# A two-layer decoder trunk on one core: six raw weight buffers, four lower ones, and a gate bias moved to another queue and to later steps

## The chip, the core and the metric

The kernel runs on one core of a Trainium2 chip. The metric is the device time of one execution in microseconds (us). The engines that matter here are TensorE (PE; its weight loads are PEld), VectorE (DVE), ScalarE (ACT), GpSimd (POOL) and SyncE (SP), which only issues DMAs. Each engine works through its own instructions in a fixed order; a DMA is issued by the queue of one of them, and an instruction that waits holds back everything behind it on its engine or queue.

## What is computed

Each of two layers normalises x (256 rows, 2048 columns), projects it with one wide matrix, feeds four branches, merges the branches under sigmoid gates and adds one output projection to x.

```python
for l in range(DEPTH):                                   # DEPTH = 2
    h = rms_norm(x, norm_g[l])
    proj = h @ w_in[l]                                   # 2048 -> 9 x 1024 + 2 x 512 + 64 + 8192
    (pv, pz, cq, ckv, kr, mz, cb, cc, cx, cz, xq, xz, gpre) = split(proj)
    y_pool = pool_mixer(pv, pool_w[l], pool_scale[l]) * silu(pz)
    y_mla  = mla_mixer(cq, ckv, kr, ...) * silu(mz)
    y_conv = conv_mixer(cb, cc, cx, conv_w[l]) * silu(cz)
    y_mem  = memory_xattn(xq, rms_norm(mem) @ w_mem_kv[l], ...) * silu(xz)
    gates  = sigmoid(gpre + gate_b[l])                   # four gates of 256 x 2048
    merged = sum(gates[:, :, i] * (y[i] @ w_branch[l, i]) for i in range(4))
    x = x + merged @ w_out[l]
```

All of it is float32. The weights are read once, and every 128 x 1024 chunk of them goes through the same preparation before TensorE uses it.

## The kernel before

**Chunks.** A weight chunk is 128 partitions by 1024 columns, 512 KB. `wchunks` (line 310) takes three buffers for it: `raw` (four of them), the upper part `hi` (five) and the lower part `lo` (five). SP loads `raw`, ScalarE rounds it into `hi` (L321), VectorE subtracts the two into `lo` (L322), and TensorE uses both parts with the activations, which are split in the same way. `tm_block` (activations as the stationary operand, L334 to L336) does three matmuls of 512 columns for each 128 rows of weight; `fm_block` and `fine_block` (weights stationary) do one of 512 columns for `hi` and one of 256 for `lo`. `fm_block` (L343) makes two 128-column halves from chunks of 256 columns by four k-tiles, and serves the projections mz and xz; `fine_block` (L373) makes one half from two chunks of 128 columns by eight k-tiles, and serves pv, pz, cc, cx, cb and cz (the names in `FINE`). A fine block's sum stands in one of two small PSUM banks, `ms`, until ScalarE has copied it out (`fmt`, L387).

**Order.** The program is written as if in one sequence; a scheduler turns it into an order for each engine, by priority and by when buffers come free. Within `tc.high_priority(n)` instructions are taken n places earlier than they stand. `lead[0]` is that n for the load, the cast and the subtraction of a chunk: `AHEAD` = 100, and `NEAR` = 40 in the stage described next. A buffer of a tag goes to the tiles of that tag one after the other, when an earlier tile's last reader is done.

**The stage of seven block products.** After the gates of the mla and mem branches the kernel computes the pool and conv branches out of 48 fine blocks (`pool_branch`, `conv_branch`). Between them it works off three other pieces of the input projection: the groups (0, 0), (0, 1) and (2, 0) of `SEVEN`, each 1024 columns of the pool or conv gate. A group is a 2 x 2 block product done with seven multiplications instead of eight (`seven`, L415). For each of eight pairs of row tiles it loads two raw chunks `ra` and `rb`, forms block differences in them in place (L457, L458, L467, L468), makes four pairs of `hi` and `lo` (casts L449, L456, L466, L476, subtraction L441), and issues seven products of three matmuls each (L432 to L434). `ra` and `rb` stay in their buffers until the last pairs that come from them are made. A group's sums fill three `acc` tiles and one `ms` bank. The generator yields after every product. Every fine block first calls `pull(RATE)` with RATE = 160/46, so three or four products are done ahead of each fine block; in the pool branch's output matmuls (`fm_tile`, L340 and L341) `pull(1)` asks for one. `drain` finishes what is left.

**End of a group.** When the last product is done, ScalarE and VectorE put the seven sums together (L485 to L492) and the generator yields True, which ends that pull. At the next pull it goes on with both halves of the group's bias: each loads 512 values of `gate_b`, broadcast to 128 rows, by SP into a `gb` tile (two buffers, L496), adds it on VectorE (L497), takes the sigmoid on ScalarE (L498), and stores the gate to DRAM by POOL's queue (`kept`, L499). `gates` later reads these back by POOL's queue (L979); the other twenty gate pieces are computed there with a `gb` load of their own on SP (L982). The tag `t2` has seven buffers of 128 x 512 for all kinds of short-lived tiles (`fmt`, `sg`, `c`, `u3`, `yp`, `mt` and others).

Of the kernel before, what the change touches and what calls it, by code (L numbers as in the profile page):

```python
# [10 lines left out]
F32 = mybir.dt.float32  # L11
F32R = mybir.dt.float32r
# [5 lines left out]
P = 128  # L18
AHEAD = 100
NEAR = 40  # L20
# [2 lines left out]
SEQUENCE = "A0 A1 F T0 F T1 S0 A2 F V0 T2 S1 A3 F V1 T3 S2 F V2 S3 F V3 X0 X1 F Y0 Y1 X2 X3 F Y2 Y3"  # L23
CK = 2
SCRATCH = 1024
FINE = ("pv", "pz", "cc", "cx", "cb", "cz")
D = 2048
S = 256
DEPTH = 2
# [2 lines left out]
KT = D // P  # L32
# [33 lines left out]
def weight_plan():  # L66
    plan, off = {}, 0

    def add(name, c0, n, nk, kt):
        nonlocal off  # L70
        plan[name, c0] = (off, n, nk, kt)
        off += P * kt * n

    def fm(name):
        if name in FINE:
            for b in range(8):
                add("in", OFF[name] + 128 * b, 128, 8, KT)
        else:
            for b in range(4):
                add("in", OFF[name] + 256 * b, 256, 4, KT)  # L80

    for e in range(4):
        add("mem_kv", 512 * e, 512, 2, KT)
    add("in", OFF["cq"], 512, 2, KT)
    for b in range(2):
        add("in", OFF["ckv"] + 288 * b, 288, 2, KT)
    for b in range(2):
        add("in", OFF["xq"] + 512 * b, 512, 2, KT)
    for hp in range(4):
        add("uq", 384 * hp, 384, 2, 4)  # L90
        add("ukv", 512 * hp, 512, 2, 4)
    for name in ("mz", "xz", "pv", "pz", "cc", "cx", "cb", "cz"):
        fm(name)
    for b in range(2):
        add("pool", 512 * b, 256, 4, 4)
    for bi in range(4):
        for e in range(4):
            if (bi, e // 2) not in SEVEN:
                add("in", OFF["gate"] + bi * D + 512 * e, 512, 2, KT)
            elif e % 2 == 0:  # L100
                add("in", OFF["gate"] + bi * D + 512 * e, 1024, 1, KT)
            add(f"br{bi}", 512 * e, 512, 2, 8)
    for e in range(4):
        add("out", 512 * e, 512, 2, KT)
    return plan, off
# [17 lines left out]
def tile_hybrid_trunk(  # L123
# [16 lines left out]
    def nm(s):  # L140
        uid[0] += 1
        return f"{s}{uid[0]}"
# [13 lines left out]
    def t2(s):  # L156
        return tp.tile([P, 512], F32, tag="t2", name=nm(s), bufs=7)
# [32 lines left out]
    def bcast_rows(v):  # L190
        return v.rearrange("(o n) -> o n", o=1).broadcast_to([P, v.shape[0]])
# [101 lines left out]
    def step():  # L293
        if background:
            run = background.pop(0)
            if run is not None:
                run()
# [7 lines left out]
            background.extend([None] * (delay - len(background)))  # L305
        background.extend(runs)

    stream, owed, lead = [], [0.0], [AHEAD]

    def wchunks(l, name, c0):  # L310
        off, n, nk, kt = plan[name, c0]
        m = nk * n
        for k0 in range(0, kt, nk):
            raw = wp.tile([P, 1024], F32, tag="raw", name=nm("raw"), bufs=4)
            hi = wp.tile([P, 1024], F32R, tag="hi", name=nm("hi"), bufs=5)
            lo = wp.tile([P, 1024], F32R, tag="lo", name=nm("lo"), bufs=5)
            o = off + P * n * k0
            step()
            with tc.high_priority(lead[0]):
                nc.sync.dma_start(raw[:, :m], weights[l, o : o + P * m].rearrange("(p m) -> p m", p=P))  # L320
                A.copy(hi[:, :m], raw[:, :m])  # L321
                V.tensor_tensor(lo[:, :m], raw[:, :m], hi[:, :m].bitcast(F32), ALU.subtract)  # L322
            yield k0, nk, kt, n, *(w[:, :m].rearrange("p (k n) -> p k n", n=n) for w in (hi, lo))
# [16 lines left out]
        T.matmul(ps[:, j, :], hi[:, k, n0 : n0 + P], o[:, half].rearrange("p a s -> p (a s)"), start=first, stop=False)  # L340
        T.matmul(ps[:, j, :S], lo[:, k, n0 : n0 + P], o[:, half, 0, :], start=False, stop=last)  # L341

    def fm_block(rhs, l, name, c0):  # L343
        ps = acc()
        for k0, nk, kt, n, hi, lo in wchunks(l, name, c0):
            for j in range(2):
                n0 = j * P
                for k in range(nk):
                    o = rhs[(k0 + k) // 2][:, k % 2].rearrange("p a s -> p (a s)")
                    T.matmul(ps[:, j, :], hi[:, k, n0 : n0 + P], o, start=k0 + k == 0, stop=False)  # L350
                for k in range(nk):
                    o = rhs[(k0 + k) // 2][:, k % 2, 0, :]
                    T.matmul(ps[:, j, :S], lo[:, k, n0 : n0 + P], o, start=False, stop=k0 + k == kt - 1)  # L353
        return ps


    def pull(n):
        owed[0] += n
        while stream and owed[0] >= 1:
            owed[0] -= 1  # L360
            done = next(stream[0], None)
            if done is None:
                stream.pop(0)
            if done:
                break

    def drain():
        while stream:
            owed[0] = 1000.0
            pull(0)  # L370
        owed[0] = 0.0

    def fine_block(rhs, l, c0):  # L373
        pull(RATE)
        ps = ms()
        for k0, nk, kt, n, hi, lo in wchunks(l, "in", c0):
            for k in range(nk):
                o = rhs[(k0 + k) // 2][:, k % 2].rearrange("p a s -> p (a s)")
                T.matmul(ps, hi[:, k, :], o, start=k0 + k == 0, stop=False)  # L379
            for k in range(nk):  # L380
                o = rhs[(k0 + k) // 2][:, k % 2, 0, :]
                T.matmul(ps[:, :S], lo[:, k, :], o, start=False, stop=k0 + k == kt - 1)  # L382
        return ps

    def fine_sum(dst, ps):
# [29 lines left out]
    def seven(l, bi, ep, h, sx):  # L415
# [5 lines left out]
        for u in range(8):  # L421
# [13 lines left out]

            def pair():
                hi = wp.tile([P, 1024], F32R, tag="hi", name=nm("hi"), bufs=5)
                return hi, wp.tile([P, 1024], F32R, tag="lo", name=nm("lo"), bufs=5)

            def lower(x, raw, cols):  # L440
                V.tensor_tensor(x[1][:, cols], raw[:, cols], x[0][:, cols].bitcast(F32), ALU.subtract)  # L441

            ra, rb = (wp.tile([P, 1024], F32, tag="raw", name=nm("raw"), bufs=4) for _ in range(2))
            with tc.high_priority(lead[0]):
                for i, r in enumerate((ra, rb)):
                    at = off + P * 1024 * (2 * u + i)
                    nc.sync.dma_start(r, weights[l, at : at + P * 1024].rearrange("(p m) -> p m", p=P))
                x = pair()
                A.copy(x[0][:, left], ra[:, left])  # L449
                lower(x, ra, left)  # L450
# [39 lines left out]
        V.tensor_tensor(c, c, bank[5], ALU.add)  # L490
        V.tensor_tensor(g[1][:, 0, :], c, bank[3], ALU.add)
        V.tensor_tensor(g[0][:, 1, :], u3, bank[4], ALU.subtract)  # L492
        yield True
        for i in range(2):
            gb = tp.tile([P, 512], F32, tag="gb", name=nm("gb"), bufs=2)
            nc.sync.dma_start(gb, bcast_rows(gate_b[l, c0 + 512 * i : c0 + 512 * (i + 1)]))  # L496
            V.tensor_tensor(g[i], g[i], gb.unsqueeze(1).broadcast_to([P, 2, 512]), ALU.add)  # L497
            A.activation(g[i], g[i], AF.Sigmoid)  # L498
            nc.gpsimd.dma_start(kept[bi, 2 * ep + i], g[i])  # L499

    def fm_sum(dst, ps):
        tmp = t2("fmt").rearrange("p (n s) -> p n s", n=2)
# [149 lines left out]
        return kT, vv  # L652

    def silu_half(z, i, h, l, c0):
        ps = fm_block(h, l, "in", c0 + 256 * i)
        sl = slice(2 * i, 2 * i + 2)
        fm_sum(z[:, sl, :], ps)
        sg = t2("sg").rearrange("p (n s) -> p n s", n=2)
        A.activation(sg, z[:, sl, :], AF.Sigmoid)
        V.tensor_tensor(z[:, sl, :], z[:, sl, :], sg, ALU.mult)  # L660
# [311 lines left out]
    def gates(l, h, ys, branch, first, last):  # L972
        bi = BRANCH_OF[branch]
        mT = []
        for e in range(4):
            c0 = bi * D + 512 * e
            g = t4("g")[:, :1024].rearrange("p (t c) -> p t c", t=2)
            if (bi, e) in kept:
                nc.gpsimd.dma_start(g, kept[bi, e])  # L979
            else:  # L980
                gb = tp.tile([P, 512], F32, tag="gb", name=nm("gb"), bufs=2)
                nc.sync.dma_start(gb, bcast_rows(gate_b[l, c0 : c0 + 512]))  # L982
                pg = tm_block(h, l, "in", OFF["gate"] + c0)
                V.tensor_tensor(g, pg, gb.unsqueeze(1).broadcast_to([P, 2, 512]), ALU.add)
                A.activation(g, g, AF.Sigmoid)
            if not first:
                mg = t4("mg")[:, :1024].rearrange("p (t c) -> p t c", t=2)
                nc.gpsimd.dma_start(mg, sums[e])
            pb = tm_block(ys, l, f"br{bi}", 512 * e)
            V.tensor_tensor(g, g, pb, ALU.mult)  # L990
            if not first:
                V.tensor_tensor(g, g, mg, ALU.add)
            if last:
                defer(transposed_operands(g, None, None, 4, mT), D_MT)
            else:
                nc.gpsimd.dma_start(sums[e], g)
        return mT
# [36 lines left out]
    for l in range(DEPTH):  # L1034
# [51 lines left out]
        flush()  # L1086
        stream += [seven(l, bi, ep, h, sx) for bi, ep in SEVEN]
        owed[0] = -RATE
        lead[0] = NEAR
        y_pool = pool_branch(l, vec, h)  # L1090
        y_conv = conv_branch(l, vec, h)
        drain()
        lead[0] = AHEAD
        gates(l, h, y_pool, "pool", False, False)
        mT = gates(l, h, y_conv, "conv", False, True)
        if l + 1 < DEPTH:
# [66 lines left out]
```

## Time and profile before

| what | us |
| --- | --- |
| time, median of 3 runs | 2507.07 (2507.02 to 2508.68) |
| time of the profiled execution | 2505.73 |
| its span, first to last instruction | 2504.0 |
| weight chunks loaded (512, 384 and 288 KB) | 836 + 16 + 32 |
| mean of a cast of 128 x 1024 (L321), whole span | 1.03 |
| mean of a subtraction of 128 x 1024 (L322), whole span | 1.20 |

In the profile an engine's busy time is the time covered by its instructions; a matmul's end is modelled, and neighbouring matmuls overlap. A row of a group gives the line, the engine, what is written from what, the count, the busy time, the mean duration in ns, and after the bar the engine's idle time just before these instructions with what ended it. A row of a wait gives who waited for whom, the total in us, the number of times and the longest. In a timeline row the first number is the start in us, the second the duration, and a bracket holds the idle time before it.

### The profile page before, as it was taken

To read this page: it belongs to the slowest core of one execution; us is meant where nothing else is said; L and a number is where in the kernel's file an instruction comes from. 1 tells how busy PE (TensorE), PEld (TensorE's weight loads), DVE (VectorE), ACT (ScalarE), POOL (GpSimd) and SP (SyncE) were. 2 spreads that over 40 slices of the span, in tenths; PEclk is the share of its full clock that TensorE was granted. 3 is DMA by queue.
4 is the path that set the end of the run, shared out by engine and by line. 5 is a ranking of instruction groups with operands and counts; after the bars stand their busy time and mean duration, and the time that the engine had idled before them with its cause. 6 is when DMAs were issued, how large, how long until landed. Compare 5 with 4: busy or idle time off the path is not lost.

```text
span 2504.0 us, 33197 instructions
## 1 busy us (share of the span) xinstructions
PE 2473.0 (99%) x12258; PEld 2080.0 (83%) x12258; DVE 1790.1 (71%) x2646; ACT 1356.9 (54%) x1881; POOL 40.4 (2%) x88
## 2 busy tenths in 40 slices
PE   8999999999999999999999999999999999999999
PEld 7888888888887888888888888888888878888887
DVE  6766787555898888766474677875558888888653
ACT  7556674444565555445454566744445655555442
POOL 0000000000000000100000000000000000001000
PEclk9999999999999999999999999999999999999999
DMA  8664436677555666886655654366766556668764
GB/s 315 218 205 160 149 127 211 213 237 234 185 198 198 201 217 204 299 291 231 219 186 163 205 164 148 124 219 219 225 222 209 193 191 199 217 217 307 246 228 144
DMA packets 154052, 522.03 MB, mean 208 GB/s; under 512 B 17312, under 2 KB 18336, under 8 KB 153888
## 3 DMA queue, kind: packets, MB, share of 16 engines
q1 hardware_dynamic: 142800, 481.06, 58.2%
q0 software_dynamic: 10368, 37.75, 4.2%
q8 instruction: 96, 1.57, 0.3%
q10 hardware_dynamic: 720, 1.09, 0.1%
q14 instruction: 68, 0.56, 0.1%
HBM read 496.76 MB, written 23.07 MB: 208 GB/s over the span
## 4 chain that ended last, share of the span: by engine, by line
PE 84%; DVE 7%; DMA 5%; ACT 2%; issue 1%; SPq 0%; DVEq 0%; ACTq 0%
PE acc L336 18%; PE acc L335 18%; PE acc L334 18%; PE ms L379 10%; DMA raw<-in_weights_dram 5%; PE ms L382 5%; PE acc L350 4%; PE acc L353 2%; DVE lo L322 2%; PE acc L433 2%; PE acc L432 2%; PE acc L434 2%; DVE lo L441 1%; ACT hi L321 1%; PE ms L873 1%
## 5 line engine op out<-in xcount | busy, mean ns | idle before, releaser
L322 DVE TENSOR_TENSOR lo<-raw,hi 128x1024 fp32r<-128x1024 f32 (+1 forms) x788 | 943.3, 1199 | 578.3 <-ACT hi L321 576.1
L321 ACT CAST hi<-raw 128x1024 fp32r<-128x1024 f32 (+1 forms) x788 | 813.1, 1033 | 900.0 <-PE acc L336 568.0
L334 PE MATMUL acc<-hi,op 128*128 128x512 f32 (+2 forms) x2112 | 812.6, 385 | 5.8 <-ACT op L558 5.8
L335 PE MATMUL acc<-lo,op 128*128 128x512 f32 (+2 forms) x2112 | 808.4, 383 | 1.9 <-DVE lo L322 1.8
L336 PE MATMUL acc<-hi,op 128*128 128x512 f32 (+2 forms) x2112 | 808.9, 383 | 0.0
L334 PEld LDWEIGHTS acc<-hi,op 128*128 128x128 f32 x2112 | 397.1, 188 | 79.4 <-ACT op L558 6.4
L335 PEld LDWEIGHTS acc<-lo,op 128*128 128x128 f32 x2112 | 397.2, 188 | 77.3 <-DVE lo L322 3.5
L336 PEld LDWEIGHTS acc<-hi,op 128*128 128x128 f32 x2112 | 396.8, 188 | 76.9 <-issue 1.3
L379 PE MATMUL ms<-op,hi 128*128 128x512 f32 x1536 | 384.9, 392 | 6.7 <-ACT fmt L387 4.8
L379 PEld LDWEIGHTS ms<-op,hi 128*128 128x128 f32 x1536 | 280.8, 188 | 68.2 <-ACT fmt L387 12.3
L441 DVE TENSOR_TENSOR lo<-raw,hi 128x512 fp32r<-128x512 f32 x192 | 206.3, 1088 | 28.2 <-ACT hi L449 12.8
L382 PEld LDWEIGHTS ms<-op,lo 128*128 128x128 f32 x1536 | 209.5, 190 | 15.0
L382 PE MATMUL ms<-op,lo 128*128 128x256 f32 x1536 | 214.1, 282 | 0.0
L350 PE MATMUL acc<-op,hi 128*128 128x512 f32 x512 | 144.3, 397 | 0.0
L350 PEld LDWEIGHTS acc<-op,hi 128*128 128x128 f32 x512 | 87.6, 189 | 11.7 <-issue 0.7
L353 PEld LDWEIGHTS acc<-op,lo 128*128 128x128 f32 x512 | 78.5, 189 | 10.7 <-issue 0.7
L353 PE MATMUL acc<-op,lo 128*128 128x256 f32 x512 | 83.8, 283 | 0.0
L433 PE MATMUL acc<-lo,sx 128*128 128x512 f32 x192 | 76.4, 398 | 6.5 <-DVE lo L441 6.5
L432 PE MATMUL acc<-hi,sx 128*128 128x512 f32 x192 | 75.5, 393 | 1.0 <-ACT hi L476 1.0
L434 PE MATMUL acc<-hi,sx 128*128 128x512 f32 x192 | 74.8, 390 | 0.0
L387 ACT COPY fmt<-ms 128x512 f32<-128x512 f32 x112 | 65.0, 580 | 6.3 <-PE ms L382 5.9
L456 ACT CAST hi<-raw 128x1024 fp32r<-128x1024 f32 x48 | 50.4, 1051 | 33.1 <-DMA raw<-in_weights_dram 15.4
(254 smaller groups left out, 1985.4 us busy)
## 6 DMA issues: line engine op xcount, KB each, us to landing
raw<-in_weights_dram SPq DMA_DIRECT2D x836, 512.0 KB, 4.3
sums<-g POOLq DMA_DIRECT2D x24, 512.0 KB, 4.5
mg<-sums POOLq DMA_DIRECT2D x24, 512.0 KB, 8.1
raw<-in_weights_dram SPq DMA_DIRECT2D x32, 288.0 KB, 2.8
gb<-in_gate_b_dram SPq DMA_DIRECT2D x32, 256.0 KB, 4.4
raw<-in_weights_dram SPq DMA_DIRECT2D x16, 384.0 KB, 3.0
kept<-g POOLq DMA_DIRECT2D x12, 512.0 KB, 6.5
g<-kept POOLq DMA_DIRECT2D x12, 512.0 KB, 6.6
```

What stands on the lines that cost most here:

```text
L321: A.copy(hi[:, :m], raw[:, :m])
L322: V.tensor_tensor(lo[:, :m], raw[:, :m], hi[:, :m].bitcast(F32), ALU.subtract)
L334: T.matmul(ps[:, t, :n], hh, hi[:, k, :], start=kk == 0, stop=False)
L335: T.matmul(ps[:, t, :n], hh, lo[:, k, :], start=False, stop=False)
L336: T.matmul(ps[:, t, :n], hl, hi[:, k, :], start=False, stop=kk == kt - 1)
L350: T.matmul(ps[:, j, :], hi[:, k, n0 : n0 + P], o, start=k0 + k == 0, stop=False)
L353: T.matmul(ps[:, j, :S], lo[:, k, n0 : n0 + P], o, start=False, stop=k0 + k == kt - 1)
L379: T.matmul(ps, hi[:, k, :], o, start=k0 + k == 0, stop=False)
L382: T.matmul(ps[:, :S], lo[:, k, :], o, start=False, stop=k0 + k == kt - 1)
L432: T.matmul(bank[i], lh[0], hi[:, cols], start=u == 0, stop=False)
L433: T.matmul(bank[i], lh[0], lo[:, cols], start=False, stop=False)
L441: V.tensor_tensor(x[1][:, cols], raw[:, cols], x[0][:, cols].bitcast(F32), ALU.subtract)
```

## The change

- `raw` has six buffers instead of four, `lo` four instead of five. The `gb` tag with its two buffers is gone, and the bias uses the seven `t2` buffers, in `gates` too.
- `lead` has two entries. `lead[1]` is the priority of the weight loads, `lead[0]` that of the casts and subtractions. Outside the stage both are 100; inside they are 80 and 40.
- The two halves of a group's bias leave the generator. They are put in a list `later`; each call of `pull` does one of them before it goes on with the products, and `drain` does what is left. Their bias is loaded by POOL's queue instead of SP's.
- The weights of mz and xz are laid out in blocks of 128 columns like those of the fine projections; `fm_block` runs the two halves one after the other by `fm_run`, which `fine_block` uses too.

```diff
     def fm(name):
-        if name in FINE:
-            for b in range(8):
-                add("in", OFF[name] + 128 * b, 128, 8, KT)
-        else:
-            for b in range(4):
-                add("in", OFF[name] + 256 * b, 256, 4, KT)
+        for b in range(8):
+            add("in", OFF[name] + 128 * b, 128, 8, KT)
...
-    stream, owed, lead = [], [0.0], [AHEAD]
+    stream, owed, lead = [], [0.0], [AHEAD, AHEAD]
...
-            raw = wp.tile([P, 1024], F32, tag="raw", name=nm("raw"), bufs=4)
+            raw = wp.tile([P, 1024], F32, tag="raw", name=nm("raw"), bufs=6)
             hi = wp.tile([P, 1024], F32R, tag="hi", name=nm("hi"), bufs=5)
-            lo = wp.tile([P, 1024], F32R, tag="lo", name=nm("lo"), bufs=5)
+            lo = wp.tile([P, 1024], F32R, tag="lo", name=nm("lo"), bufs=4)
             o = off + P * n * k0
             step()
+            with tc.high_priority(lead[1]):
+                nc.sync.dma_start(raw[:, :m], weights[l, o : o + P * m].rearrange("(p m) -> p m", p=P))
             with tc.high_priority(lead[0]):
-                nc.sync.dma_start(raw[:, :m], weights[l, o : o + P * m].rearrange("(p m) -> p m", p=P))
                 A.copy(hi[:, :m], raw[:, :m])
                 V.tensor_tensor(lo[:, :m], raw[:, :m], hi[:, :m].bitcast(F32), ALU.subtract)
...
-    def fm_block(rhs, l, name, c0):
+    def fm_run(ps, rhs, l, c0):
+        for k0, nk, kt, n, hi, lo in wchunks(l, "in", c0):
+            for k in range(nk):
+                o = rhs[(k0 + k) // 2][:, k % 2].rearrange("p a s -> p (a s)")
+                T.matmul(ps, hi[:, k, :], o, start=k0 + k == 0, stop=False)
+            for k in range(nk):
+                o = rhs[(k0 + k) // 2][:, k % 2, 0, :]
+                T.matmul(ps[:, :S], lo[:, k, :], o, start=False, stop=k0 + k == kt - 1)
+
+    def fm_block(rhs, l, c0):
         ps = acc()
-        for k0, nk, kt, n, hi, lo in wchunks(l, name, c0):
-            for j in range(2):
-                ...
+        for j in range(2):
+            fm_run(ps[:, j, :], rhs, l, c0 + P * j)
         return ps
 
+    later = []
 
     def pull(n):
         owed[0] += n
+        if later:
+            later.pop(0)()
         while stream and owed[0] >= 1:
...
         owed[0] = 0.0
+        while later:
+            later.pop(0)()
...
-            ra, rb = (wp.tile([P, 1024], F32, tag="raw", name=nm("raw"), bufs=4) for _ in range(2))
-            with tc.high_priority(lead[0]):
+            ra, rb = (wp.tile([P, 1024], F32, tag="raw", name=nm("raw"), bufs=6) for _ in range(2))
+            with tc.high_priority(lead[1]):
                 for i, r in enumerate((ra, rb)):
                     at = off + P * 1024 * (2 * u + i)
                     nc.sync.dma_start(r, weights[l, at : at + P * 1024].rearrange("(p m) -> p m", p=P))
+            with tc.high_priority(lead[0]):
                 x = pair()
...
-        yield True
-        for i in range(2):
-            gb = tp.tile([P, 512], F32, tag="gb", name=nm("gb"), bufs=2)
-            nc.sync.dma_start(gb, bcast_rows(gate_b[l, c0 + 512 * i : c0 + 512 * (i + 1)]))
+
+        def finish(i):
+            gb = t2("gb")
+            nc.gpsimd.dma_start(gb, bcast_rows(gate_b[l, c0 + 512 * i : c0 + 512 * (i + 1)]))
             V.tensor_tensor(g[i], g[i], gb.unsqueeze(1).broadcast_to([P, 2, 512]), ALU.add)
             A.activation(g[i], g[i], AF.Sigmoid)
             nc.gpsimd.dma_start(kept[bi, 2 * ep + i], g[i])
+
+        later.extend([lambda: finish(0), lambda: finish(1)])
+        yield True
...
-                gb = tp.tile([P, 512], F32, tag="gb", name=nm("gb"), bufs=2)
+                gb = t2("gb")
                 nc.sync.dma_start(gb, bcast_rows(gate_b[l, c0 : c0 + 512]))
...
-        lead[0] = NEAR
+        lead[:] = [NEAR, 2 * NEAR]
         y_pool = pool_branch(l, vec, h)
         y_conv = conv_branch(l, vec, h)
         drain()
-        lead[0] = AHEAD
+        lead[:] = [AHEAD, AHEAD]
```

More of the change, by code (lines that the diff above doesn't have):

```diff
@@ L25 @@
 SCRATCH = 1024
-FINE = ("pv", "pz", "cc", "cx", "cb", "cz")
 D = 2048
@@ L341, in fm_tile @@
         T.matmul(ps[:, j, :S], lo[:, k, n0 : n0 + P], o[:, half, 0, :], start=False, stop=last)
-    def fm_block(rhs, l, name, c0):
-        ps = acc()
-        for k0, nk, kt, n, hi, lo in wchunks(l, name, c0):
-            for j in range(2):
[L347 to L353, printed above, removed]
+    def fm_run(ps, rhs, l, c0):
[7 more added lines that the diff above has]
+    def fm_block(rhs, l, c0):
+        ps = acc()
+        for j in range(2):
+            fm_run(ps[:, j, :], rhs, l, c0 + P * j)
         return ps
+    later = []
     def pull(n):
         owed[0] += n
+        if later:
+            later.pop(0)()
         while stream and owed[0] >= 1:
@@ L375, in fine_block @@
         ps = ms()
[L376 to L382, printed above, removed]
+        fm_run(ps, rhs, l, c0)
         return ps
@@ L437, in pair @@
                 hi = wp.tile([P, 1024], F32R, tag="hi", name=nm("hi"), bufs=5)
-                return hi, wp.tile([P, 1024], F32R, tag="lo", name=nm("lo"), bufs=5)
+                return hi, wp.tile([P, 1024], F32R, tag="lo", name=nm("lo"), bufs=4)
             def lower(x, raw, cols):
                 V.tensor_tensor(x[1][:, cols], raw[:, cols], x[0][:, cols].bitcast(F32), ALU.subtract)
-            ra, rb = (wp.tile([P, 1024], F32, tag="raw", name=nm("raw"), bufs=4) for _ in range(2))
-            with tc.high_priority(lead[0]):
+            ra, rb = (wp.tile([P, 1024], F32, tag="raw", name=nm("raw"), bufs=6) for _ in range(2))
+            with tc.high_priority(lead[1]):
                 for i, r in enumerate((ra, rb)):
@@ L654, in silu_half @@
     def silu_half(z, i, h, l, c0):
-        ps = fm_block(h, l, "in", c0 + 256 * i)
+        ps = fm_block(h, l, c0 + 256 * i)
         sl = slice(2 * i, 2 * i + 2)
```

## Prediction

> **What bounds the kernel now.** I read the page first, then the table of windows over the whole span, then the timeline, the waits and the DMA issues inside the one stage where the windows show gaps.
>
> ```profile
> span 2504.0 us, 33197 instructions
> ...
> PE 2473.0 (99%) x12258; PEld 2080.0 (83%) x12258; DVE 1790.1 (71%) x2646; ACT 1356.9 (54%) x1881; POOL 40.4 (2%) x88
> ```
>
> TensorE is busy in 2473 of 2504 us, so anything that only keeps it better fed can win about 31 us. The windows (span; then busy time of PE, PEld, DVE, ACT and POOL, granted clock, DMA share, GB/s) say where. The first two rows are the stage of the seven block products in layer 1 and layer 2:
>
> ```profile
> 629.00:1031.00 402.00, 392.94 (x2075) 334.21 (x2074) 348.94 (x447) 232.33 (x275) 4.83 (x13) 1.00 0.62 205
> 1876.00:2278.00 402.00, 393.75 (x2077) 334.96 (x2076) 349.24 (x447) 233.97 (x276) 4.84 (x13) 1.00 0.62 205
> ```
> ```profile
> 375.00:400.00 25.00, 25.00 (x112) 20.70 (x111) 24.84 (x56) 13.24 (x16) 0.00 (x0) 1.00 0.55 176
> 750.00:775.00 25.00, 22.31 (x120) 18.65 (x119) 22.66 (x31) 14.49 (x19) 1.18 (x3) 1.00 0.60 199
> ```
>
> Idle time of PE in the two stages is 9.06 + 8.25 = 17.3 us, over half of all there is, at a full clock. At 375 VectorE is busy for 24.84 of 25 us and PE still has no gap; at 750 VectorE is less busy and PE loses 2.69 us. PE's modelled ends hide part of a gap, so I size the loss by the pace of undisturbed steps, from the timeline of PE (start, duration, line; the row at 1875.97 is from the chain of waits):
>
> ```profile
> 629.33 1.98 PE L379 MATMUL ms<-op,hi 128*128 128x512 f32 x8
> ...
> 634.89 0.40 PE L432 MATMUL acc<-hi,op 128*128 128x512 f32 x1
> ...
> 636.96 1.98 PE L379 MATMUL ms<-op,hi 128*128 128x512 f32 x8
> ```
> ```profile
> 763.27 0.40 PE L340 MATMUL ms<-op,hi 128*128 128x512 f32 x1
> ...
> 763.62 0.40 PE L340 MATMUL ms<-op,hi 128*128 128x512 f32 x1
> ```
> ```profile
> 1031.10 0.40 PE L334 MATMUL acc<-hi,op 128*128 128x512 f32 x1
> ```
> ```profile
> 1875.97 1.81 PE ms L379 x8
> ```
> ```profile
> 2276.84 0.40 PE L334 MATMUL acc<-hi,op 128*128 128x512 f32 x1
> ```
>
> A fine block takes 634.89 - 629.33 = 5.56 us, three products 636.96 - 634.89 = 2.07, so 0.69 each, a pool pair 0.35. The code asks for 48 fine blocks, 3 x 56 products and 16 pool pairs a layer: 266.9 + 115.9 + 5.6 = 388.4 us. The stages last 1031.10 - 629.33 = 401.8 and 2276.84 - 1875.97 = 400.9, so **the loss is 13.4 + 12.5 = 25.9 us**. That is all the change can win here. What ended the weight loads' idle time in layer 1 (us, times, longest):
>
> ```profile
> PEld ms L379 <- ACT fmt L387: 6.4, 9, 1.8
> PEld acc L433 <- DVE lo L441: 5.1, 5, 2.0
> PEld ms L340 <- ACT fmt L387: 2.2, 4, 1.6
> PEld ms L379 <- ACT hi L321: 1.6, 1, 1.6
> PEld acc L432 <- ACT hi L476: 0.8, 1, 0.8
> ```
>
> ScalarE ended 11.0 of 16.1, 68%, and VectorE's lower parts 32%. Of 25.9 us that makes **17.6 behind ScalarE and 8.3 behind VectorE**. And ScalarE itself waited, in the same stage:
>
> ```profile
> ACT hi L321 <- DMA raw<-in_weights_dram: 54.8, 37, 4.0
> ...
> ACT hi L449 <- DMA raw<-in_weights_dram: 14.2, 11, 2.1
> ACT hi L456 <- DMA raw<-in_weights_dram: 7.6, 7, 2.2
> ...
> ACT hi L476 <- DVE raw L468: 6.4, 5, 2.8
> ...
> ACT hi L466 <- DVE raw L458: 4.1, 3, 1.5
> ```
>
> 76.6 us for raw weights, 10.5 for VectorE's block differences. One stall shows the link, a cast waiting 3.50 us for its load with the copy that frees the fine block's bank queued behind it:
>
> ```profile
> 941.30 1.05 ACT L321 CAST hi<-raw 128x1024 fp32r<-128x1024 f32 x1 [3.50 <-DMA raw<-in_weights_dram]
> ...
> 944.69 0.58 ACT L387 COPY fmt<-ms 128x512 f32<-128x512 f32 x1
> ...
> 945.32 1.88 PE L379 MATMUL ms<-op,hi 128*128 128x512 f32 x7 [1.40 <-ACT fmt L387]
> ```
>
> And why loads are late, from the waits of SP's queue in this stage, the DMA issues and the groups by line:
>
> ```profile
> SPq L320 <- DVE lo L322: 128.5, 66, 5.8
> ...
> SPq L496 <- DVE g L497: 13.3, 4, 9.0
> ```
> ```profile
> raw<-in_weights_dram SPq DMA_DIRECT2D x836, 512.0 KB, 4.3
> ...
> gb<-in_gate_b_dram SPq DMA_DIRECT2D x32, 256.0 KB, 4.4
> ...
> kept<-g POOLq DMA_DIRECT2D x12, 512.0 KB, 6.5
> ```
> ```profile
> L322 DVE TENSOR_TENSOR lo<-raw,hi 128x1024 fp32r<-128x1024 f32 x100 | 121.9, 1222 | 38.3 <-ACT hi L321 37.7
> ...
> L497 DVE TENSOR_TENSOR g<-g,gb 128x1024 f32<-128x1024 f32 x4 | 4.9, 1218 | 0.0
> ```
> ```profile
> L321 ACT CAST hi<-raw 128x1024 fp32r<-128x1024 f32 x101 | 106.1, 1051 | 109.5 <-DMA raw<-in_weights_dram 54.8 <-PE ms L379 45.2 <-DVE lo L441 3.2
> ```
>
> SP mostly waits for a raw buffer, which the lower part releases; the DMA engines are at 0.62, so bandwidth is not what is short.
>
> **Six raw buffers, loads 80 places ahead.** A step is one fine block and 3.48 products, 5.56 + 2.40 = 7.96 us, and needs three loads: two of the fine block and on average one of the products' pairs (two loads for seven products). A fine load holds its buffer 4.3 + 1.05 + 1.22 = 6.6 us. The products' first buffer lives on over three products, the second over five, on average 4/3.48 of a step or 9.1 us more: 15.7. So a step asks for 2 x 6.6 + 15.7 = 28.9 buffer-us of 4 x 7.96 = 31.8, 91%; six buffers offer 47.8, and 60% are used. At 91% a late lower part becomes a late load at once; at 60% it need not. The loads' priority alone would do little with four buffers, since SP already waits for buffers; with six it lets SP use them. If every raw wait vanished, 76.6 of 87.1 parts of the 17.6 us would go, 15.5. If the casts then only queue behind VectorE, nothing goes. I take 12, nearer the upper end, because VectorE has 402 - 348.9 = 53 us of idle time in the stage to run ahead in, though at 388 us it would be 90% busy and some queues stay.
>
> **Bias on POOL's queue, in two later steps.** The bias loads of the next group stand in SP's queue until L497 frees a bias buffer: 13.3 us in layer 1, 9.0 at once, in which the raw loads behind cannot issue. That block goes; its worth is part of the 12. It adds two loads a group to POOL, which is busy 4.83 of 402 us; queued behind them are the stores of the gates and later reads of them. The second load need not stand behind the first store, since it depends on nothing but a buffer. If it does, the store is issued after the first step's sigmoid, and a landing of 6.5 us (the POOL stores' row) still fits nearly a full step of 7.96, but not the short pool steps. Then VectorE would wait in front of L497 with all its lower parts behind, up to 6.5 us at the second add of each of six groups, 39 us; at the other end nothing. I take nothing, as the four adds of the L497 row waited 0.0 behind SP's 4.4 us, and the load may go early. The second add, sigmoid and store come a step later; their readers, the gates of the pool and conv branches, come after the stage, and the last group's after the four pool blocks, so nobody waits. VectorE's own work stays, but one add of 1.22 us leaves each group's burst: at most 6 x 1.22 = 7.3 of the 8.3 us, at least nothing. I take 2, since the burst before 768 contains much else.
>
> A rule speaks against this move. POOL's DMA instructions here took, all twelve stores together with their range:
>
> ```profile
> L499 POOL DMA_DIRECT2D kept<-g x12: 531/534/553, 766.2 to 2286.8; - x12
> ```
>
> The Trainium skill, "SBUF — State Buffer", section "SBUF: two separate sides", says that VectorE's two-port modes lock GpSimd out of writing descriptors for DMAs from its queue, and the section after it gives about 620 ns growing to about 3100. By that a bias would land 2.5 us later, an estimate from the same page of the Trainium skill, and twelve of them could cost VectorE 30 us. The trace does not bear it out: 531 to 553 ns, with VectorE 87% busy around them (nearly all of it tensor_tensor, which the page gives no two-port mode), so it adds nothing to the sum.
>
> **Four lower buffers instead of five.** VectorE may now run four parts ahead of PE, so a lower part can wait for PE with VectorE's sums and differences queued behind. A part is a quarter of a step, 2.0 us of PE. The nearest row, a lower part waiting for PE in this stage, is small:
>
> ```profile
> DVE lo L441 <- PE ms L382: 1.3, 1, 1.3
> ```
>
> If each of the ten places where PE waits for L441 (five a layer) grew by one part, that is 20 us; if VectorE never is four parts ahead, nothing. I take 2, near that row.
>
> **The rest.** The mz and xz weights in 128 columns make the same matmuls and loads of the same size; eight upper products instead of four now stand before the first lower one, which only helps. Nothing, unless VectorE's full windows (375 above) get worse, and there PE has no gap. The bias in the shared t2 buffers: nothing in the gate stages, where four to seven buffers replace two; between -1.5 and +1.5 at the start, where six loads instead of four go ahead of the rows. I take 0.
>
> **Sum**: -12 - 2 + 2 = -12 us. The profiled execution took 2505.73, its span 2504.0 with 1.7 around it, the median is 2507.07; I subtract from the median: **2495 us**. About 5 us (0.2%) is what a measurement of this kernel can tell from no change.
>
> **Rivals.** *VectorE is the limit.* It is busy 348.94 us of a stage that PE could do in 388.4, and some stalls end at L441 directly. Earlier raws then only move ScalarE's waits from loads to lower parts, and 17.6 + 8.3 shrinks by 2 or 3 us: 2504. Against it: 76.6 us of waits for loads, and VectorE idle for 53 us mostly because the cast came late (37.7 us at L322). The Trainium skill, "Perfetto Trace Analysis", section "Identifying the Most-Contended Engine", takes the engine with the highest occupancy as the one to work on and judges TensorE by its weight loads; here that is VectorE, 87% against PEld's 83%, and by that rule this rival wins. Chance 0.18.
>
> *The extra buffers are taken by the products.* Two of six hold one pair, and at 80 places ahead the next pair takes two more, so the fine blocks again live on two. Then about half is won: 2501. Chance 0.12.
>
> *Slower: four lower parts.* VectorE, in order, stands before a lower part whose buffer PE still holds, and the fine sums and block differences behind it come late. It decides as soon as VectorE falls more than three parts (6 us) behind rather than four (8 us), as in the bursts near 768. The price is up to 20 us at the ten places; with half of it, and only 4 won from the loads, 2507 - 4 + 10 = 2513. Chance 0.12.
>
> *Nearly all of the loss goes*: 25.9 - 4 = 22, 2485. Chance 0.08.
>
> **Numbers.** The forecast has the remaining 0.50. Faster: 0.50 + 0.12 + 0.08 = 0.70. Same: 0.18. Slower: 0.12. The range 2485 to 2506 takes in all but the slower rival and the far edges; on the fast side it ends with the last rival.
>
> **What would show it.** Right: the two stages shrink from 402 to about 396 us each, the rows "hi from DMA raw" fall from 76.6 to under 30, no bias is left in SP's queue, PE's waits for the fmt copy fall to a few us, and waits for L441 stay. Wrong: new rows of lower parts waiting for PE, of L497 waiting for the bias, or gaps in the windows outside the two stages.

## The result, and the profile after

| kernel | median us | runs |
| --- | --- | --- |
| before | 2507.88 (2507.02 to 2509.55) | 4 |
| changed | 2490.2 (2488.44 to 2491.89) | 4 |

The ratio is 0.9926, 95% interval 0.9911 to 0.9941: 17.7 us faster, where 12 were forecast, inside the range. On a second chip, where the kernel before took 2512.32, the changed kernel (run `a_again`) took 2489.56: 0.9912, interval 0.9899 to 0.9925, a gain of 22.8 us. All ratios below are against the kernel before on the same chip. The only profile of the kernel before is of the first chip, so a difference between its stages and those of a run elsewhere may hold a few us of the chip.

In the changed kernel the casts and subtractions of `wchunks` are L317 and L318 (before: L321, L322), its load L315 (L320), the fine matmuls L343 and L346 (L379, L382), the products L429 to L431, the products' loads L444, their subtraction L438 (L441), the last cast L474 (L476), the differences L455, L456, L465 and L466, the bias load L494 and its add L495 (L496, L497), the copy of a fine sum L384 (L387).

The timeline of PE gives the borders of the two stages, four single rows that answer to the four of the prediction:

```profile
629.52 1.98 PE L343 MATMUL ms<-op,hi 128*128 128x512 f32 x8
...
1025.07 0.40 PE L330 MATMUL acc<-hi,op 128*128 128x512 f32 x1
...
1868.29 1.07 PE L343 MATMUL ms<-op,hi 128*128 128x512 f32 x4
...
2261.26 0.40 PE L330 MATMUL acc<-hi,op 128*128 128x512 f32 x1
```

Counted in the same way, from its first fine matmul, the second stage before starts at 1875.81, not at the 1875.97 that the prediction took from the chain, and lasts 401.0 us:

```profile
1875.81 1.98 PE L379 MATMUL ms<-op,hi 128*128 128x512 f32 x8
```

The stages now last 395.6 and 393.0 us instead of 401.8 and 401.0. Of the 16.0 us by which the span shrank (2504.0 to 2488.0), 14.3 came from there. The first stage starts where it did (629.52 against 629.33). The windows of the two stages, columns as before:

```profile
629.00:1025.00 396.00, 391.75 (x2076) 334.90 (x2075) 347.65 (x446) 232.83 (x275) 8.22 (x19) 1.00 0.63 208
1868.00:2262.00 394.00, 392.00 (x2079) 335.41 (x2078) 348.25 (x447) 233.65 (x276) 8.22 (x19) 1.00 0.63 210
```

PE's idle time in them fell from 17.3 to 4.25 + 2.00 = 6.3 us. VectorE did the same work, 348 us, in less time. The waits in the first stage:

```profile
ACT hi L317 <- PE ms L343: 46.8, 41, 1.8
...
DVE lo L318 <- PE ms L346: 19.9, 19, 1.6
...
ACT hi L474 <- DVE raw L466: 12.6, 6, 3.5
...
PEld ms L343 <- ACT fmt L384: 5.4, 6, 2.8
...
ACT hi L317 <- DMA raw<-in_weights_dram: 2.3, 2, 1.2
```

ScalarE's 76.6 us of waits for raw weights are 2.3 (9.1 in `a_again`). Over all its casts it now waits 102 us for PE to give back a buffer, where it was 64 before, which means that it is ahead more often. VectorE's subtractions wait for PE too, 19.9 us, a row that was not there before. Of the weight loads' waits the largest row is still that for the copies of the fine sums (5.4), and one stall, at 921, is half of it:

```profile
916.45 1.05 ACT L317 CAST hi<-raw 128x1024 fp32r<-128x1024 f32 x1 [1.17 <-DMA raw<-in_weights_dram]
...
921.92 1.04 ACT L317 CAST hi<-raw 128x1024 fp32r<-128x1024 f32 x1 [4.43 <-PE acc L430]
922.88 1.04 ACT L454 CAST hi<-raw 128x1024 fp32r<-128x1024 f32 x1
923.82 0.58 ACT L384 COPY fmt<-ms 128x512 f32<-128x512 f32 x1
```

The copy stands behind two casts. The chain of waits has a raw load from 915.90 to 922.85 just ahead of the second, 6.95 us where the median is 4.3. The gates' stores had been issued at 905.69 and 910.90 and a read of one at 914.20; that they slowed this load is likely, not shown.

### The profile page after: what moved, and what is told of

It reads as the page before. It is cut to its first block, busy times and chain, and to the rows that moved or that the text cites. A ratio compares the mean times of both kernels' runs of the same rounds, so it can differ in the third digit from the quotient of the medians.

```text
span 2488.0 us, 33641 instructions
## 1 busy us (share of the span) xinstructions
PE 2470.4 (99%) x12258; PEld 2083.1 (84%) x12258; DVE 1791.3 (72%) x2646; ACT 1355.3 (54%) x1881; POOL 47.2 (2%) x100
## 4 chain that ended last, share of the span: by engine, by line
PE 96%; DVE 2%; DMA 1%; issue 1%; ACT 0%; SPq 0%; DVEq 0%; ACTq 0%
PE acc L330 19%; PE acc L332 19%; PE acc L331 19%; PE ms L343 13%; PE ms L346 7%; PE acc L343 5%; PE acc L346 2%; PE acc L430 2%; PE acc L429 2%; PE acc L431 2%; DMA raw<-in_weights_dram 1%; PE ms L874 1%; PE ms L873 1%; PE ms L517 1%; DVE lo L438 1%
## 5 line engine op out<-in xcount | busy, mean ns | idle before, releaser
L318 DVE TENSOR_TENSOR lo<-raw,hi 128x1024 fp32r<-128x1024 f32 (+1 forms) x788 | 941.8, 1199 | 577.8 <-PE acc L331 420.5
L317 ACT CAST hi<-raw 128x1024 fp32r<-128x1024 f32 (+1 forms) x788 | 811.0, 1033 | 798.2 <-PE acc L332 557.6
L330 PEld LDWEIGHTS acc<-hi,op 128*128 128x128 f32 x2112 | 397.8, 188 | 80.8 <-ACT op L559 6.7
L332 PEld LDWEIGHTS acc<-hi,op 128*128 128x128 f32 x2112 | 397.5, 188 | 76.4 <-DVE op L560 0.7
L343 PE MATMUL ms<-op,hi 128*128 128x512 f32 x1536 | 385.1, 392 | 5.2 <-ACT fmt L384 3.9
L343 PEld LDWEIGHTS ms<-op,hi 128*128 128x128 f32 x1536 | 281.4, 188 | 64.4 <-ACT fmt L384 8.1
L438 DVE TENSOR_TENSOR lo<-raw,hi 128x512 fp32r<-128x512 f32 x192 | 206.3, 1088 | 23.6 <-PE ms L346 10.5
L346 PEld LDWEIGHTS ms<-op,lo 128*128 128x128 f32 x1536 | 209.5, 191 | 16.2 <-DVE lo L318 1.4
L346 PE MATMUL ms<-op,lo 128*128 128x256 f32 x1536 | 214.5, 283 | 0.5 <-DVE lo L318 0.5
L343 PE MATMUL acc<-op,hi 128*128 128x512 f32 x512 | 135.0, 398 | 0.0
L343 PEld LDWEIGHTS acc<-op,hi 128*128 128x128 f32 x512 | 90.9, 189 | 16.2 <-issue 1.3
L429 PE MATMUL acc<-hi,sx 128*128 128x512 f32 x192 | 75.8, 395 | 0.5 <-ACT hi L474 0.5
L454 ACT CAST hi<-raw 128x1024 fp32r<-128x1024 f32 x48 | 50.5, 1052 | 44.9 <-PE ms L343 24.7
L431 PE MATMUL acc<-hi,sx 128*128 128x512 f32 x192 | 75.0, 390 | 0.0
L346 PEld LDWEIGHTS acc<-op,lo 128*128 128x128 f32 x512 | 70.2, 190 | 5.0
L474 ACT CAST hi<-raw 128x1024 fp32r<-128x1024 f32 x48 | 50.4, 1050 | 43.8 <-DVE raw L466 25.4
L346 PE MATMUL acc<-op,lo 128*128 128x256 f32 x512 | 73.1, 283 | 0.0
```

Source lines behind the costliest of these rows:

```text
L330: T.matmul(ps[:, t, :n], hh, hi[:, k, :], start=kk == 0, stop=False)
L332: T.matmul(ps[:, t, :n], hl, hi[:, k, :], start=False, stop=kk == kt - 1)
L429: T.matmul(bank[i], lh[0], hi[:, cols], start=u == 0, stop=False)
L431: T.matmul(bank[i], lh[1], hi[:, cols], start=False, stop=u == 7)
L454: A.copy(x[0], rb)
```

## The experiments

My theory: the six raw buffers bring nearly all of the gain, the four lower ones cost a little, the bias edits bring a little. The rivals: that the bias leaving SP's queue, the loads' priority, the layout of mz and xz, or the end of VectorE's burst brings it; and that four lower buffers cost much.

| run | ratio | 95% interval | stages, us |
| --- | --- | --- | --- |
| `a_again`, the changed kernel | 0.9912 | 0.9899 to 0.9925 | 397.3, 393.4 |
| `a_raw4` | 1.0049 | 1.0037 to 1.0061 | 415.6, 409.7 |
| `a_raw4_lead40` | 1.0056 | 1.0043 to 1.0069 | 414.0, 410.1 |
| `a_lead40` | 0.9911 | 0.9898 to 0.9924 | 397.8, 393.5 |
| `a_gbsp` | 0.9938 | 0.9926 to 0.9950 | 399.6, 397.8 |
| `a_onestep` | 0.9938 | 0.9926 to 0.9949 | 397.1, 397.3 |
| `b_lo4` | 1.0074 | 1.0059 to 1.0088 | 411.3, 415.5 |
| `b_bufs` | 0.9937 | 0.9925 to 0.9949 | 398.1, 397.5 |
| `a_raw5_lo5` | 0.9931 | 0.9919 to 0.9944 | 399.3, 396.3 |
| `a_raw6_lo5` | 0.9923 | 0.9910 to 0.9935 | 391.8, 391.6 |
| `a_fm256` | 0.9913 | 0.9900 to 0.9927 | 398.0, 393.0 |
| `a_spread` | 0.9897 | 0.9880 to 0.9913 | 394.0, 393.5 |

The stages are read from PE's timeline like those above. Names with `a_` start from the changed kernel, with `b_` from the one before.

One thing besides the waits moves these times by a few us: single stretches of 3.4 us in which TensorE's granted clock was at half. The stall near 922 shows it, in two executions of the same kernel. First `a_again`, its PE row behind the stall and the window from there (columns as before, the clock is the third number from the end):

```profile
922.35 3.58 PE L343 MATMUL ms<-op,hi 128*128 128x512 f32 x8 [2.46 <-ACT fmt L384]
```
```profile
922.20:925.60 3.40, 3.25 (x8) 2.58 (x9) 3.27 (x4) 1.99 (x3) 0.00 (x0) 0.50 0.51 161
```

Then the same from the changed kernel's first profile:

```profile
924.45 2.12 PE L343 MATMUL ms<-op,hi 128*128 128x512 f32 x8 [2.36 <-ACT fmt L384]
```
```profile
922.20:925.60 3.40, 1.15 (x5) 0.97 (x6) 2.39 (x3) 3.40 (x5) 0.00 (x0) 1.00 0.40 151
```

At half the clock the eight matmuls took 3.58 us instead of 2.12, and the first stage 397.3 instead of 395.6. One such stretch costs about 1.7 us, an estimate: half of 3.4. Leaving out the first 300 us and the last 20 of each profile, every such stretch stands at or just behind 1.9 to 3.3 us of idle time of PE, in one gap or two close together. The reverse does not hold: of 20 gaps of 2.0 us or more, 15 are followed by one. The profiles of the kernel before, the changed kernel and `a_spread` have none there, `a_again`, `a_lead40`, `a_fm256` and `a_raw4_lead40` one, `a_onestep`, `b_bufs` and `a_raw4` two, `a_gbsp` three, `a_raw5_lo5` as much as three, `b_lo4` four. A difference of 2 or 3 us between the stages of two runs can be that alone.

**Raw buffers back to four** (`a_raw4`).

```diff
-tag="raw", name=nm("raw"), bufs=6
+tag="raw", name=nm("raw"), bufs=4
```

> The changed kernel with four raw buffers again; all else as changed (four lower ones, loads 80 places ahead, bias on POOL's queue in two steps). Theory (the raw buffers bring the gain): nearly all of it is lost, about 2504 us, the two stages of block products return to about 401 us each, and ScalarE waits again some 50 to 80 us a stage for raw loads. Rival (the bias leaving SP's queue brings it): at least two thirds of the gain stay, 2496 us or less.

2522.65 against 2511.54: not only is the gain lost, the kernel is 11 us slower than before. The raw waits are back, in the first stage:

```profile
ACT hi L317 <- DMA raw<-in_weights_dram: 86.7, 59, 6.2
...
PEld ms L343 <- ACT fmt L384: 21.9, 21, 3.0
```

So the raw buffers are worth about 33 us within the change (against `a_lead40`, 2489.31 beside it), and something else in it costs, which was not in my theory.

**Loads 40 places ahead** (`a_lead40`: `lead[:] = [NEAR, NEAR]`).

> The changed kernel with the loads only 40 places ahead in the stage, as before; six raw buffers stay. Theory (buffers first, priority second): half of the gain or more stays, 2492 to 2499 us, since SP issues a load as soon as a buffer is free in any case. Rival (the priority is what counts): back to 2502 us or more.

2489.31, ratio 0.9911 against 0.9912 for the changed kernel: all of the gain stays, more than the theory had. The priority is worth nothing. SP's waits say why: with 40 places it waits for the same releases for the same time as with 80 (first fence `a_lead40`, second the changed kernel):

```profile
SPq L444 <- DVE lo L318: 119.6, 27, 9.0
SPq L315 <- DVE lo L438: 74.0, 39, 11.1
SPq L315 <- DVE lo L318: 56.5, 33, 6.2
```
```profile
SPq L444 <- DVE lo L318: 118.5, 27, 9.1
SPq L315 <- DVE lo L438: 76.6, 40, 11.1
SPq L315 <- DVE lo L318: 54.8, 33, 6.0
```

**Four raw buffers and 40 places** (`a_raw4_lead40`), to see whether the priority is what costs with few buffers.

> The changed kernel with four raw buffers and the loads 40 places ahead; it keeps four lower buffers, the bias on POOL in two steps and the new mz and xz layout. With four raw buffers and 80 places the stages were 14 and 9 us longer than in the kernel before. Theory (at 80 places the products' pairs take the few buffers early and starve the fine blocks): most of that goes away, the stages come back to 396 to 402 us and the ratio to 0.995 to 1.000. Rival (four lower buffers are what costs): it stays near 1.005 and the stages above 408 us.

2525.03: no. The theory named there falls, the rival stands.

**Four lower buffers alone** (`b_lo4`: `lo` from `bufs=5` to `bufs=4` in the kernel before).

> The kernel before with four lower buffers instead of five and nothing else. Theory (the four lower buffers are nearly free): ratio 1.000 to 1.002, stages within 3 us of 401.8 and 401.0. Rival (they cost, and the raw buffers buy it back): 1.004 or more, stages above 406 us.

2530.35 against 2512.32, 18 us slower. The first stage of that kernel:

```profile
ACT hi L321 <- DMA raw<-in_weights_dram: 92.5, 62, 4.7
...
ACT hi L476 <- DVE raw L468: 14.6, 7, 3.1
PEld ms L379 <- ACT fmt L387: 14.1, 18, 2.0
...
DVE lo L322 <- PE ms L382: 9.0, 8, 1.6
```

Subtractions wait 9.0 us for PE, which holds the lower buffers (the row is missing in the kernel before), and ScalarE's wait for raw weights grows from 54.8 to 92.5 on that line. The two can be linked by the raw buffer: it is given back when the subtraction ends. I matched the k-th load, cast and subtraction of the fine blocks in layer 1's stage (101 of them) and took means, in us:

| kernel | landing to cast | cast to subtraction | buffer held |
| --- | --- | --- | --- |
| before (4 raw, 5 lower) | 1.10 | 0.47 | 8.1 |
| `b_lo4` (4, 4) | 0.62 | 1.02 | 8.3 |
| changed (6, 4) | 4.71 | 2.05 | 13.7 |
| `a_raw6_lo5` (6, 5) | 5.92 | 0.64 | 13.3 |

With four raw buffers a loaded chunk lies ready for 1.10 us on average before ScalarE takes it. With four lower buffers the subtraction starts 0.55 us later, and the chunk lies ready 0.48 us less; that further delay then reaches PE is my reading of these means. With six, chunks lie ready for 4.71 us, and a subtraction may wait 2 us. There is a second path: VectorE works in order, so the block differences behind a waiting subtraction come late as well, and ScalarE's waits for them doubled (10.5 to 20.9 us). They are as long in the changed kernel (22.7), which is faster, so they alone do not cost the time; but no run separates the two paths. Part of the 18 us can be the clock: this execution has four stretches at half, about 7 us by the estimate above.

**The buffers alone** (`b_bufs`: the kernel before with six raw and four lower buffers and `gb = t2("gb")` in both places).

> The kernel before with only the buffers of the change: six raw, four lower, the bias in the seven shared ones; the loads stay 40 places ahead, the bias on SP's queue with both halves at one step, mz and xz as before. Theory (the raw buffers bring most, the bias's queue and steps 4 to 7 us of it): ratio 0.995 to 0.997. Rival (buffers bring all): 0.993 or less. Rival (the bias edits bring it): 0.999 or more.

2495.81, ratio 0.9937, between the theory and the rival: 16.5 us of the 22.8 that the whole change brings on that chip (2512.32 to 2489.56). The bias edits, priority and layout share the other 6. Which waits went shows what each part does. In the first stage of `b_bufs` the rows behind ScalarE's copies and casts are halved, from 11.0 to 5.5 us, and the row behind VectorE's lower parts is nearly what it was, 4.4 after 5.1:

```profile
PEld acc L433 <- DVE lo L441: 4.4, 4, 2.5
PEld ms L379 <- ACT fmt L387: 3.4, 5, 1.9
PEld ms L340 <- ACT fmt L387: 1.5, 6, 0.4
...
PEld acc L432 <- ACT hi L476: 0.6, 1, 0.6
```

**Five and five** (`a_raw5_lo5`: the same space).

> The changed kernel with five raw and five lower buffers: the same space, split the other way. With four raw buffers, taking the lower ones from five to four cost 18 us; with six raw and four lower the time is 0.9912 to 0.9926. Theory (a lower part that waits for its buffer holds its raw buffer, so the two kinds are one row of places and their sum counts): within 4 us of the changed kernel, 0.990 to 0.993. Rival (only the number of raw buffers counts): half-way between four and six of them, 0.996 to 1.000.

2495.3, ratio 0.9931, at the theory's edge and clearly not at the rival's 0.996. Raw and lower buffers can stand in for each other. Six and four are no worse; their stages are 2 to 4 us shorter, but this run had 10 us of half clock in its stages (about 5 us by the estimate above), so no order between the two is shown.

**Six and five** (`a_raw6_lo5`). To make room, `t2` gets six tiles instead of seven and takes in the scratch tile of `sumsq`.

```diff
-tag="lo", name=nm("lo"), bufs=4
+tag="lo", name=nm("lo"), bufs=5
...
-        return tp.tile([P, 512], F32, tag="t2", name=nm(s), bufs=7)
+        return tp.tile([P, 512], F32, tag="t2", name=nm(s), bufs=6)
...
-        j = tp.tile([P, 512], F32, tag="junk", name=nm("junk"), bufs=1)
+        j = t2("junk")
```

> The changed kernel with five lower buffers again beside the six raw ones; the space comes from the shared short-lived tiles, six instead of seven of them, which also take in the scratch tile of the sums of squares. Theory (one place more, where few are missing): 2 to 5 us faster than the changed kernel, 0.989 to 0.991. Rival (with six raw buffers the fifth lower one is worth nothing, as VectorE is the limit): 0.991 to 0.993. Should the short-lived tiles be missed, it is slower, above 0.994.

2493.02, ratio 0.9923: as a whole no better, as the rival had it, but the parts differ. The stages last 391.8 and 391.6 us, the shortest of all runs, 3.4 us above the 388.4 of undisturbed steps. The time was lost ahead of them: the mla gates start at 379.95 instead of 372.45, and among PE's waits up to there is one that doubled, with 6.8 us of half clock at and behind it (first `a_raw6_lo5`, then the changed kernel):

```profile
PEld acc L330 <- ACT op L559: 13.2, 3, 6.6
```
```profile
PEld acc L330 <- ACT op L559: 6.7, 2, 5.7
```

L559 makes the operands out of the memory tokens and x at the start, from `t2` tiles. So the fifth lower buffer is still worth about 5 us in the stages; a place for it that costs nothing was not found, and not tried further.

**The bias on SP's queue again** (`a_gbsp`: `nc.sync.dma_start(gb, ...)` in `finish`).

> The changed kernel with a group's bias loaded by SP again, still from the seven shared buffers and in two steps. Theory: no difference that can be measured, 2488 to 2493 us, since the bias tile no longer waits for L497 and so does not block SP's queue for long. Rival (SP's queue is the point): SP waits again 9 us or more at a bias load and the time is 2496 us or more.

2496.51, some 7 us slower than `a_lead40` beside it, which was as fast as the changed kernel. But not as the rival says: SP's queue does not wait at L494 at all. What changed is VectorE's order at the end of the first group (rows of `a_gbsp`, then of the changed kernel):

```profile
762.96 1.22 DVE L495 TENSOR_TENSOR g<-g,gb 128x1024 f32<-128x1024 f32 x1
764.10 0.69 DVE L466 TENSOR_TENSOR raw<-raw 128x512 f32<-128x512 f32 x1
```
```profile
764.92 0.69 DVE L466 TENSOR_TENSOR raw<-raw 128x512 f32<-128x512 f32 x1
...
765.52 1.23 DVE L495 TENSOR_TENSOR g<-g,gb 128x1024 f32<-128x1024 f32 x1
```

With the load on SP the scheduler puts the bias add ahead of the difference L466, which the cast L474 and then PE wait for; on POOL's queue it puts it behind. PE stands idle for 1.36 and 0.76 us there, against 0.45 and 0.26 in the changed kernel; the same gaps come in the second layer, and a stretch of half clock behind them each time. Against `a_lead40` PE idles 2.3 us more in the two stages and has two such stretches more (about 3.4 us): together 5.7 of the 6.2 us by which the stages are longer. That the order is the cause is read from these places, not shown alone.

**Both halves in one step** (`a_onestep`: `later.append(lambda: (finish(0), finish(1)))`).

> The changed kernel with both halves of a group's bias in the first of the two later steps. Theory: 1 to 2 us slower than the changed kernel, 2491 to 2492 us, the whole of it at the ends of the groups. Rival (the burst of VectorE at a group's end is what stalled PE): 4 us slower or more, 2494 us and up, with PE waiting for the lower parts L438 again.

2495.95, 6.6 us slower than `a_lead40`: the rival. VectorE does two adds in a row, and PE waits for the subtraction behind them:

```profile
764.70 2.35 DVE L495 TENSOR_TENSOR g<-g,gb 128x1024 f32<-128x1024 f32 x2
...
768.58 0.28 PEld L430 LDWEIGHTS acc<-lo,sx 128*128 128x128 f32 x1 [2.47 <-DVE lo L438]
```

The same gap comes in the second layer, and half clock behind both.

**The old layout of mz and xz** (`a_fm256`: blocks of 256 columns and the old `fm_block` in the changed kernel).

> The changed kernel with the mz and xz weights in 256 columns by four k-tiles and their matmuls in the old order. Theory: no difference that can be measured, 0.991 to 0.993. Rival (the longer runs of equal matmuls are a gain of their own): 0.994 or more, with the time lost ahead of the gates and not in the two stages.

2490.34: nothing.

**The bias further apart** (`a_spread`).

```diff
-        later.extend([lambda: finish(0), lambda: finish(1)])
+        later.extend([lambda: None, lambda: finish(0), lambda: None, lambda: finish(1)])
```

> The changed kernel with an empty step ahead of each half of a group's bias, so that the halves come in the second and the fourth step instead of the first and the second. Doing both in one step cost about 6 us. Theory (what is left at the ends of the groups is a crowd of VectorE's work and of the gates' stores and reads on the DMA engines, and each step apart thins it): 1 to 4 us faster than the changed kernel, 0.9895 to 0.9915, with the stall of 2.4 us near 922 smaller. Rival (two steps are enough and the rest is VectorE's own load): 0.9912 to 0.9926, with the stall in its place.

2485.5 against 2511.03, ratio 0.9897: the fastest run, though its interval (0.9880 to 0.9913) overlaps the changed kernel's. The first stage is 394.0 us, the second 393.5, no shorter than without the empty steps. The stall near 922 is a little smaller, 1.84 us after 2.36, as the theory has it, and has no half clock behind it:

```profile
921.84 2.11 PE L343 MATMUL ms<-op,hi 128*128 128x512 f32 x8 [1.84 <-ACT fmt L384]
```

**The changed kernel again** (`a_again`), told above.

> The changed kernel itself once more, beside the others of this call. Both theories: 0.991 to 0.994 of the kernel before.

## Why the prediction was right, and where it was not

- **The place, right.** All but 2 us of the profiled gain came from the two stages, which shrank to 395.6 and 393.0 where 396 was forecast, raw waits fell from 76.6 to under 30 (2.3), and no group's bias is left in SP's queue. The 388.4 us of undisturbed steps is a floor that `a_raw6_lo5` nearly reaches. One sign failed: the waits for the fmt copies fell only from 8.6 to 6.6 us in the first stage and from 8.9 to 3.9 in the second.
- **The number, partly luck.** The forecast of 12 us is two thirds of the 17.7 measured and about half of the 22.8 on the second chip, which is what the rival with a chance of 0.08 forecast (22). Inside a range of 21 us it holds because the errors of the next two terms partly cancel.
- **Six raw buffers, 12 us: mis-sized.** With four lower buffers they are worth 34.5 us (`b_lo4` to `b_bufs`, with the bias's shared buffers among it). The estimate that a fine load holds its buffer for 6.6 us (from a cast of 1.05 us and a subtraction of 1.22; the 1.03 and 1.20 of the table before are means with smaller chunks among them) left out the waiting before and behind the cast: 8.1 us measured. That the stages were nearly out of buffers (91%) was right, and understated. That six would be used to 60% was not: SP still waits for a buffer before most loads (the `a_lead40` rows), a fine load holds its own for 13.7 us, and the slack is the 4.71 us for which its chunk lies ready.
- **Four lower buffers, 2 us: the step that failed.** They cost 18 us alone, with four raw buffers, and about 5 in the stages with six (`a_raw6_lo5`). I priced a wait of PE for the lower part, and took a small row (1.3 us) as the nearest. The price is paid elsewhere, as far as the means above show it: a subtraction that waits keeps its raw buffer. Raw and lower buffers are one chain (`a_raw5_lo5`), and I summed them as two terms. The errors of the two partly cancel: -10 forecast for both, -16.5 measured (`b_bufs`). The new row of lower parts waiting for PE, named as a sign of being wrong, did come (19.9 us), and with six raw buffers it did little harm.
- **80 places ahead, wrong by half.** That it does nothing with four buffers held (`a_raw4` and `a_raw4_lead40`); that six let SP use it did not (`a_lead40`).
- **The bias, 2 us: mis-sized, and for a partly wrong reason.** Neither edit brings anything by itself: 0.9937 without both (`b_bufs`), 0.9938 with the steps alone (`a_gbsp`), 0.9938 with POOL's queue alone (`a_onestep`), and 0.9912 with both. Each of the three leaves 2.1 to 2.2 us of idle time of PE at the end of the first group in both layers, with half clock behind it. The 13.3 us block of SP that I credited was a matter of the two bias buffers, not of the queue: with shared buffers SP does not wait there.
- **PE's waits for VectorE's lower parts: I said they would stay.** They fell from 5.1 to 0.2 us in the first stage:

```profile
PEld acc L430 <- DVE lo L438: 0.2, 1, 0.2
```

- **Late loads were not the cause of those waits,** since the buffers alone left 4.4 of them. The two adds in a row were a large part of it, since with both halves in one step (`a_onestep`) they are 4.0 again, and VectorE's total of 348 us was the same all along. Over both stages the rows behind VectorE's lower parts fell by 8.5 us and those behind ScalarE by 6.2, where I had put 2 and 12. The buffers alone took 10.8 from ScalarE's rows and nothing from VectorE's, so each part of the change did act where I had put it.

- **The rival that VectorE is the limit falls, as far as its total goes.** It is busy 347.65 of 396 us, 88%, and PE idles for 4.25. The Trainium skill, "Perfetto Trace Analysis", section "Identifying the Most-Contended Engine", would have had one work on the engine of highest occupancy, VectorE; here the larger part, 16.5 of 22.8 us, came from buffers for an engine that was waiting for loads, and the rest from the order of VectorE's work, with its amount unchanged.
- **The rival that the products take the extra buffers falls too.** Half of the gain was to be left; the fine chunks lie ready for 4.71 us, and the priority of the loads changes nothing.
- **Nothing for the rest: right.** The first stage starts 0.2 us later, and 2.2 earlier in `a_again`, no more than two profiles of one kernel differ; the layout brings nothing.

## What to carry to other kernels

Count the buffers of a load-cast-subtract-use chain together: a buffer is held until the last reader behind it has found its own, so taking one away at the end of the chain can starve its beginning, and a row of late loads can be the sign of a missing output buffer. Before raising the priority of a load, look at what its queue waits for: where it waited for a buffer, priority moved nothing here. A burst at the end of a group can stall PE even when its engine has 12% to spare; here it took both edits, the step and the queue, to take the stall away. And before a difference of 2 or 3 us is explained by a wait, look at the granted clock behind the stalls.

## What the runs showed of the hardware

The bias loads on GpSimd's queue, under a VectorE that was busy for 88% of the stage, took a steady 551 to 558 ns to issue and landed in 5.8 us. SP's twenty bias loads in the same kernel landed in 5.5, and the same twelve from SP's queue in 4.9 in `a_gbsp` and 4.3 before:

```profile
L494 POOL DMA_DIRECT2D gb<-in_gate_b_dram x12: 551/556/558, 746.6 to 2250.4; - x12
```
```profile
DMA to landing us min/median/max: 3.3/5.8/6.5
```

No sign shows of the lock that the Trainium skill, "SBUF — State Buffer", describes in its section "SBUF: two separate sides"; VectorE's work here was nearly all tensor_tensor. The landings are 0.3 to 1.5 us later than SP's, and what makes that difference is open.

Behind idle time of PE of about 2 us the granted clock was at half for 3.4 us in most cases, not in all (the rows after the table of runs).
